# Forgetting attention in a two-layer trunk: page loads spread over two heads' iterations each, and all loads of the loop issued by SyncE

## The chip, the cores and the metric

The kernel runs on one core of a Trainium2 chip. The metric is the device time of one execution in microseconds (us), lower is better. Five engines matter here: TensorE (PE, matmuls and transposes), VectorE (DVE), ScalarE (ACT), GpSimd (POOL) and SyncE (SP, which only issues DMAs here). DMAs can be issued by SP, ACT or POOL; each of these engines works through its own instructions in order, so that an instruction that waits holds up everything behind it on the same engine. The transfers themselves run on 16 DMA engines.

## What is computed

One inference step of a decoder with two layers, for a prompt of 512 tokens and a group of 8 sample sequences with 4 new tokens each. Every layer is a feed-forward block, a mixer and another feed-forward block; the first layer's mixer is gated linear attention, the second's is forgetting attention (FoX) with 16 heads of 64. Only the FoX attention is touched. Its prompt half and its sample half are:

```python
def fox_prompt_attend(q, k, v, logf):          # per block of 128 queries
    s = einsum('bqhd,bkhd->bhqk', qi, k) * HD ** -0.5
    s = s + (Fi[:, :, :, None] - Ft[:, :, None, :])       # F = cumsum(logf)
    s = where(kpos <= qpos, s, -inf)
    return einsum('bhqk,bkhd->bqhd', softmax(s), v)

def fox_paged_attend(q, k_new, v_new, logf_new, cache_k, cache_v, cache_logf, page_table):
    kp = cache_k[page_table]                   # 2 pages of 128 tokens per sequence
    vp = cache_v[page_table]
    ...
    p = softmax(concat([s_past, s_new]))
    return p[..., :P] @ vp + p[..., P:] @ v_new
```

## The kernel before

The kernel is written with a tile framework: the program names tiles, each tile belongs to a tag with a fixed number of buffers, and a planner inserts all waits, hands out the buffers of a tag and sets the order of the instructions on each engine from the program's order and from when it thinks each instruction can start. So the order on an engine is close to the program's, with later work pulled ahead where earlier work can't start yet.

The function `fox` (L1159) first makes queries and gates with matmuls (`fg`, the last of these before the loop), and then runs the attention loop (L1388 to L1413) of 18 iterations `i`. Iteration `i` handles prompt head `i`; `kb = i // 2` is the pair of heads that share a 128-row slice of keys and queries. Four iterations make a sample group `p`, with `q = i % 4` counting within it; group `p` covers the sample sequences `b = 2p` and `2p + 1`.

For the prompt heads:

- `pair_loads(kb)` (L1318) loads, for a pair of heads, the values `vq` (from `vscr`, 256 KB, issued by SP), the keys twice into `kd` (from `khscr`, two DMAs of 256 KB, issued by POOL), the low parts of the keys with the decay rows `kl` (74 partitions, 296 KB, from `klscr`, by POOL) and the query-side decay rows `qe` (10 partitions, 40 KB, from `qxscr`, by POOL; named `qx` in the code). `kd`, `kl` and `qe` are of the type float32r, and the sources are float32. It also splits the queries into high and low parts (ACT, POOL).
- `head_probs(hd)` (L1336) makes the scores in PSUM (matmuls `fs`, L1348 to L1350), the row minimum (DVE, L1351), the exponential (ACT, L1352) and the scaling (DVE, L1357).
- `head_turn` (L1360) transposes the probabilities on PE (`pT`) and copies them out; `head_values(kb)` (L1376) multiplies them with `vq` (`fo`), then DVE, ACT and POOL turn the result into the high and low parts for the output projection (POOL: `ul`, L1385).

For the sample sequences:

- `pair_keys(p, s2)` (L1219) loads the two key pages of one sequence (`kp`, 512 KB each) and its two value pages (`vp`, 512 KB each), both by SP, transposes the key pages on PE (`kpT`), copies the transposes to SBUF (DVE, ACT), and returns a function `scores` that does the score matmuls `sp` (L1262).
- `pair_softmax` (L1266), `pair_probs` (L1281, transposes `spT`), `pair_values` (L1291, matmuls `so` that read `vp`) and `pair_out` (L1309) follow.

The buffers that decide when a load may start: tag `hi` has 6 buffers. One is held through the loop by the sample queries; every `kd` takes one, from its load to the last `fs` of its two heads; every `pair_keys` takes two for the transposed pages `kpT`, until its `scores`. Tag `lo` has 6, four of them held by the gates, so two remain for the `kp` of one sequence. Tag `raw` has 4: the `vp` of one group. `vq`, `kl` and `qe` have two buffers each. All these buffers are given back by PE instructions.

In the loop of the kernel before, a group's `pair_keys` run at `q = 0` and `q = 1`, the scores at `q = 1` and `q = 2`, the softmax at `q = 2`, `pair_probs` at `q = 3` and `pair_values` at the next group's `q = 0`. `pair_loads` for the next pair stands at the start of every even iteration. After the loop comes the output projection `fwo`, whose weights (`rfwo`) take over the `raw` buffers.

Of the kernel before, what the change touches and what calls it, by code (L numbers as in the profile page):

```python
# [9 lines left out]
F32 = mybir.dt.float32  # L10
# [8 lines left out]
P = 128  # L19
D = 1024  # L20
NB = 8
# [29 lines left out]
KX = 74  # L51
# [48 lines left out]
def trunk_kernel(ctx: ExitStack, tc: tile.TileContext, a, out, dbg=None, stop=None):  # L100
    nc = tc.nc
    V, S, G, PE, SP = nc.vector, nc.scalar, nc.gpsimd, nc.tensor, nc.sync
# [17 lines left out]
    def raw_tile(name, dt=F32):  # L120
        return wp.tile([P, 1056], dt, tag="raw", name=name, bufs=4)
# [191 lines left out]
    for k in range(NB):  # L313
        ps = mm_bank(f"xT{k}")
# [6 lines left out]
    ps = mm_bank("xTs")  # L321
# [694 lines left out]
    pages = [SP.value_load(pt[0:1, i:i + 1], min_val=0, max_val=npg - 1) for i in range(16)]  # L1016
# [142 lines left out]
    def fox(after_half):  # L1159
        W = a["fox_w_qg"][0]  # L1160
        with ExitStack() as es:
# [43 lines left out]
            fa = es.enter_context(tc.tile_pool(name="foxa", bufs=1))  # L1205
            xp = es.enter_context(tc.tile_pool(name="foxp", bufs=1, space=bass.MemoryType.PSUM))
            ps = aux_bank("cq")
# [7 lines left out]
            cv = a["cache_v"].rearrange("n t h d -> n t (h d)")  # L1215

            pst = {}

            def pair_keys(p, s2):  # L1219
                if s2 == 0:  # L1220
                    qx = qx2[:, (p % 2) * 512:(p % 2) * 512 + 512]
                    for par in range(2):
                        r = slice(64 * par, 64 * par + 64)
                        for kb in range(2):
                            for i in range(2):
                                o = 16 * kb + 8 * i + 4 * par
                                b = 2 * p + i
                                V.tensor_copy(out=qx[r].rearrange("p (s j k c) -> p s k j c", s=2, j=4, k=2)[:, i, kb, :, o:o + 4],
                                              in_=qTs[r, kb::2, 4 * b:4 * b + 4])
                    ps = xp.tile([P, 512], F32, tag="sp", name=f"sp{p}")  # L1230
                    PE.matmul(ps[:, 0:260], lhsT=cf[:, F_SEL + 128 * p:F_SEL + 128 * p + 128], rhs=nf[:], start=True, stop=False)
                    pst[p] = [qx, ps, []]
                qx, ps, vv = pst[p]
                b = 2 * p + s2
                kr = []
                for g in range(2):
                    t = lo_tile(f"kp{b}_{g}", F32)
                    SP.dma_start(out=t[:, 0:D], in_=ck[bass.ds(pages[2 * b + g], 1)].rearrange("o t d -> t (o d)"))
                    kr.append(t)
                for g in range(2):  # L1240
                    t = raw_tile(f"vp{b}_{g}")
                    SP.dma_start(out=t[:, 0:D], in_=cv[bass.ds(pages[2 * b + g], 1)].rearrange("o t d -> t (o d)"))
                    vv.append(t)
                kt = [hi_tile(f"kpT{b}_{i}", F32)[:, 0:1040].rearrange("p (k c) -> p k c", k=4) for i in range(2)]
                for q in range(4):
                    pk = aux_bank(f"kpT{b}_{q}")
                    for i in range(2):
                        for g in range(2):
                            PE.transpose(pk[:, i * 256 + g * P:i * 256 + (g + 1) * P], kr[g][:, (2 * q + i) * P:(2 * q + i + 1) * P], ident)
                    d = kt[q // 2][:, 2 * (q % 2):2 * (q % 2) + 2, 0:256]  # L1250
                    if q % 2:
                        S.copy(d, pk[:].rearrange("p (k c) -> p k c", k=2))
                    else:
                        V.tensor_copy(out=d, in_=pk[:].rearrange("p (k c) -> p k c", k=2))
                for i in range(2):
                    V.tensor_copy(out=kt[i][:, :, 256:260], in_=kTs[:, 4 * i:4 * i + 4, 4 * b:4 * b + 4])

                def scores():
                    for kb in range(2):
                        for j in range(4):  # L1260
                            c = (s2 * 4 + j) * 2 + kb
                            PE.matmul(ps[32 * j:32 * j + 32, 0:260], lhsT=qx[:, 32 * c:32 * c + 32], rhs=kt[j // 2][:, 2 * (j % 2) + kb],  # L1262
                                      start=False, stop=s2 == 1 and kb == 1)
                return scores

            def pair_softmax(p):  # L1266
                qx, ps, vv = pst[p]
                x = tmp.tile([P, 260], F32, tag="acc", name=f"sx{p}", bufs=2)
                sm = fa.tile([P, 4], F32, tag="sm", name=f"sm{p}", bufs=2)
                V.tensor_tensor_reduce(out=x[:], in0=ps[:, 0:260], in1=cf[:, F_NEWM:F_NEWM + 260], scale=1.0, scalar=-3.0e38, op0=ALU.add, op1=ALU.max, accum_out=sm[:, 0:1])  # L1270
                c = cq[:, p:p + 1]
                V.tensor_tensor(out=sm[:, 1:2], in0=sm[:, 0:1], in1=c, op=ALU.add)
                V.tensor_tensor(out=sm[:, 2:3], in0=c, in1=sm[:, 1:2], op=ALU.subtract)
                S.activation(x[:], x[:], AF.Exp, bias=sm[:, 2:3], accum_out=sm[:, 3:4])
                V.reciprocal(out=sm[:, 0:1], in_=sm[:, 3:4])
                V.tensor_scalar(out=x[:], in0=x[:], scalar1=sm[:, 0:1], scalar2=None, op0=ALU.mult)
                xn = tmp.tile([P, 32, 4], F32, tag="acc", name=f"xn{p}", bufs=2)
                V.tensor_tensor(out=xn[:], in0=x[:, 256:260].unsqueeze(1).to_broadcast([P, 32, 4]), in1=cf[:, F_SEQR + 32 * p:F_SEQR + 32 * p + 32].unsqueeze(2).to_broadcast([P, 32, 4]), op=ALU.mult)
                pst[p] += [x, xn]
# [35 lines left out]

            hst = {}

            def pair_loads(kb):  # L1318
                vq = fa.tile([P, 4, P], F32, tag="vq", name=f"vq{kb}", bufs=2)
                SP.dma_start(out=vq[:], in_=vscr[:].rearrange("(t p) d -> p t d", p=P)[:, :, kb * P:(kb + 1) * P])  # L1320
                kd = hi_tile(f"kd{kb}")[:, 0:1024].rearrange("p (e t) -> p e t", e=2)
                for g in range(2):
                    G.dma_start(out=kd[64 * g:64 * g + 64], in_=khscr[kb * P:(kb + 1) * P].rearrange("(e p) t -> p e t", e=2))
                kl = fa.tile([KX, 2, TP], F32R, tag="kl", name=f"kl{kb}", bufs=2)
                G.dma_start(out=kl[:], in_=klscr[2 * kb:2 * kb + 2].rearrange("e p t -> p e t"))
                qx = fa.tile([KX, 2, TP], F32R, tag="qe", name=f"qe{kb}", bufs=2)
                G.dma_start(out=qx[64:KX], in_=qxscr[2 * kb:2 * kb + 2].rearrange("e p t -> p e t"))
                qs = (uh[:, kb, 0:TP], ul[:, kb, 0:TP])
                for e in range(2):
                    r, x = slice(64 * e, 64 * e + 64), slice(64 - 64 * e, 128 - 64 * e)  # L1330
                    S.copy(qs[e][r], qT[r, kb])
                    (G if kb else V).tensor_tensor(out=qs[e][x], in0=qT[r, kb], in1=qs[e][r].bitcast(F32), op=ALU.subtract)
                    S.copy(qx[0:64, e], qT[r, kb])
                hst["v", kb], hst["k", kb] = vq, (kd, kl, qs, qx)

            def head_probs(hd):  # L1336
                kb, hh = divmod(hd, 2)
# [49 lines left out]
            sc_ = {}  # L1387
            for i in range(18):  # L1388
                p, q = divmod(i, 4)
                if i == 0:  # L1390
                    pair_loads(0)
                if i % 2 == 0 and i < 14:
                    pair_loads(i // 2 + 1)
                if i < 16:
                    head_probs(i)
                if p and q == 0:
                    pair_values(p - 1)
                if p < 4 and q == 0:
                    sc_[0] = pair_keys(p, 0)
                if p < 4 and q == 1:  # L1400
                    sc_[0]()
                    sc_[1] = pair_keys(p, 1)
                if i >= 3 and i % 2:
                    head_values((i - 3) // 2)
                if p < 4 and q == 2:
                    sc_[1]()
                    pair_softmax(p)
                if 1 <= i < 17:
                    head_turn(i - 1)
                if p < 4 and q == 3:  # L1410
                    pair_probs(p)
                if p and q == 1:
                    pair_out(p - 1)  # L1413
# [55 lines left out]
```

## Time and profile before

| | |
|---|---|
| runs shown | 2469.25, 2464.47, 2458.25 us; median 2464.47 |
| the profiled execution | 2457.02 us, its span 2455.2 us (1.8 us lie around it) |
| PE busy in it | 2391.8 us, 97% |
| attention loop in it | from 1841.7 us (first `fs`) to 1988.3 us (first matmul of `fwo`): 146.6 us |
| mean granted TensorE clock | 0.987 |

How to read it: the span runs from the first to the last instruction, and all times of the trace count from its start. The time of an engine is its busy time. PE's matmuls overlap in the pipe, so a PE that shows 98% has no gap, but that does not tell its peak. The clock that the throttle grants TensorE is given as a share of full speed. "Idle before" an instruction is put down to what released it last. A DMA's landing is the time from its issue until its semaphore tells that all of it has arrived.

### The profile page before, as it was taken

The numbers are of one execution on the slowest core, as the hardware profiler recorded it, in microseconds if no ns is written. First come the engines' busy times: TensorE is split into PE (matmuls) and PEld (weight loads), VectorE is DVE, ScalarE is ACT, GpSimd is POOL, SyncE is SP. The second block draws the span as 40 slices with busy tenths as digits, with TensorE's granted clock in tenths as the row PEclk, the third lists the DMA queues.
The fourth block names the chain that finished last, engine by engine and source line by source line (L and its number), as shares of the span: only waits on it lengthen the run. The fifth ranks groups of instructions, "written<-read, shape, count | busy, mean of one in ns | idle before, by whom it ended". The sixth has DMA issues, their size and how long they took to land. (4 is left out here: it accounts for less than half of the span.)

```text
span 2455.2 us, 48218 instructions
## 1 busy us (share of the span) xinstructions
PE 2391.8 (97%) x20204; PEld 2244.9 (91%) x20204; DVE 1237.1 (50%) x2823; ACT 783.2 (32%) x1431; POOL 293.0 (12%) x448
## 2 busy tenths in 40 slices
PE   8999999999899999999999999999998899999999
PEld 6999999988879999999879999999895589999999
DVE  6343334547656354444585444434848556444433
ACT  3212222344534222222335222222347444222221
POOL 0000000104301010000220000001325120000000
PEclk8999999999999999999999999999999899999999
DMA  8636444313172636445257322322148642222221
GB/s 296 214 123 223 162 159 157 97 48 93 38 223 71 226 126 232 157 170 170 106 149 221 104 77 85 104 86 70 53 106 206 168 125 77 87 92 90 72 84 55
DMA packets 325519, 319.38 MB, mean 130 GB/s; under 512 B 24607, under 2 KB 276349, under 8 KB 325254
## 3 DMA queue, kind: packets, MB, share of 16 engines
q1 hardware_dynamic: 297958, 293.81, 37.6%
q0 software_dynamic: 13776, 11.87, 2.3%
q10 hardware_dynamic: 13568, 10.62, 1.4%
q8 instruction: 159, 2.61, 0.4%
q14 instruction: 58, 0.48, 0.1%
HBM read 298.17 MB, written 18.38 MB: 129 GB/s over the span
## 5 line engine op out<-in xcount | busy, mean ns | idle before, releaser
L176 PE MATMUL pa<-uh,hua 128*128 128x272 f32 x1408 | 409.9, 291 | 1.6 <-ACT uh L386 1.5
L177 PE MATMUL pa<-ul,hua 128*128 128x272 f32 x1408 | 408.2, 290 | 0.4 <-DVE ul L387 0.2
L178 PE MATMUL pb<-uh,lub 128*128 128x272 f32 x1408 | 407.6, 289 | 0.0
L178 PE MATMUL pa<-uh,lua 128*128 128x272 f32 x1408 | 406.9, 289 | 0.0
L176 PE MATMUL pd<-gh,hwd 128*128 128x272 f32 x1408 | 406.8, 289 | 0.0
L177 PE MATMUL pb<-ul,hub 128*128 128x272 f32 x1408 | 405.8, 288 | 0.0
L176 PE MATMUL pb<-uh,hub 128*128 128x272 f32 x1408 | 405.7, 288 | 0.0
L178 PE MATMUL pd<-gh,lwd 128*128 128x272 f32 x1408 | 405.4, 288 | 0.0
L177 PE MATMUL pd<-gl,hwd 128*128 128x272 f32 x1408 | 405.2, 288 | 0.0
L393 DVE SCALAR_TENSOR_TENSOR h<-pd,mods,h 128x272 f32<-128x272 f32 (+1 forms) x384 | 185.0, 482 | 251.0 <-PE pd L178 249.9
L176 PEld LDWEIGHTS pa<-uh,hua 128*128 128x128 f32 x1408 | 265.8, 189 | 14.5 <-issue 6.0
L177 PEld LDWEIGHTS pa<-ul,hua 128*128 128x128 f32 x1408 | 266.0, 189 | 1.6 <-DVE ul L387 1.6
L176 PEld LDWEIGHTS pd<-gh,hwd 128*128 128x128 f32 x1408 | 265.2, 188 | 1.7 <-issue 1.6
L177 PEld LDWEIGHTS pb<-ul,hub 128*128 128x128 f32 x1408 | 266.3, 189 | 0.0
L178 PEld LDWEIGHTS pb<-uh,lub 128*128 128x128 f32 x1408 | 266.1, 189 | 0.0
L176 PEld LDWEIGHTS pb<-uh,hub 128*128 128x128 f32 x1408 | 266.0, 189 | 0.0
L178 PEld LDWEIGHTS pa<-uh,lua 128*128 128x128 f32 x1408 | 265.8, 189 | 0.0
L177 PEld LDWEIGHTS pd<-gl,hwd 128*128 128x128 f32 x1408 | 265.5, 189 | 0.0
L178 PEld LDWEIGHTS pd<-gh,lwd 128*128 128x128 f32 x1408 | 265.4, 189 | 0.0
L446 DVE TENSOR_TENSOR g<-g,pb 128x272 f32<-128x272 f32 x176 | 77.0, 437 | 349.1 <-PE pb L178 347.7
L157 ACT CAST hua<-rua 128x1024 fp32r<-128x1024 f32 x88 | 92.2, 1048 | 459.9 <-PE pd L177 349.6
L398 POOL TENSOR_TENSOR h<-h,gs 128x32 f32<-128x32 f32 x192 | 70.7, 368 | 1234.2 <-DVE gs L396 1228.8
(497 smaller groups left out, 4176.3 us busy)
## 6 DMA issues: line engine op xcount, KB each, us to landing
adaw<-in_w_ada_dram SPq DMA_DIRECT2D x128, 512.0 KB, 6.2
rua<-in_w_ffn_up_dram SPq DMA_DIRECT2D x88, 512.0 KB, 3.8
rub<-in_w_ffn_up_dram SPq DMA_DIRECT2D x88, 512.0 KB, 3.9
rwd<-in_w_ffn_down_dram SPq DMA_DIRECT2D x88, 512.0 KB, 4.9
adah<-in_w_ada_dram SPq DMA_DIRECT2D x16, 512.0 KB, 7.7
adaw<-in_w_ada_kv_dram SPq DMA_DIRECT2D x16, 512.0 KB, 7.3
s<-in_state_gla_dram SPq DMA_DIRECT2D x16, 512.0 KB, 4.7
kp<-in_cache_k_dram SPq DMA_DIRECT2D x16, 512.0 KB, 4.7
```

Source lines behind the costliest of these rows:

```text
L157: S.copy(hi, src)
L176: PE.matmul(ps, lhsT=wh, rhs=xh, start=first and i == 0, stop=False)
L177: PE.matmul(ps, lhsT=wh, rhs=xl, start=False, stop=False)
L178: PE.matmul(ps, lhsT=wl, rhs=xh, start=False, stop=last and i == n - 1)
L393: V.scalar_tensor_tensor(out=h[:, m, t0:p1], in0=ps[:, 0:n], scalar=mods[:, gate + m, 0:1], in1=h[:, m, t0:p1], op0=ALU.mult, op1=ALU.add)
L398: G.tensor_tensor(out=h[:, m, TP:T], in0=h[:, m, TP:T], in1=st[:], op=ALU.add)
L446: V.tensor_tensor(out=g[:], in0=g[:], in1=pb[:, 0:HA], op=ALU.mult)
```

## The change

- The loads `kd`, `kl` and `qe` are issued by SP instead of POOL. Their destinations are written as float32 (`bitcast`), so that source and destination have one type.
- `vq` leaves `pair_loads`: it is loaded by `value_load`, for pairs 0 and 1 at the start, and then for the next but one pair right after the `head_values` that gives its buffer back.
- The value pages leave `pair_keys`: `pair_pages(p, s2)` loads them one iteration later, at `q = 1` and `q = 3`.
- The second sequence of a group has its `pair_keys` at `q = 2` instead of `q = 1`. Its scores and the group's softmax move from `q = 2` to the start of `q = 3`, ahead of that iteration's `head_probs`. `pair_probs`, `pair_values` and `pair_out` stay where they were.

```diff
-                qx, ps, vv = pst[p]
+                qx, ps, _ = pst[p]
                 b = 2 * p + s2
                 kr = []
                 for g in range(2):
                     t = lo_tile(f"kp{b}_{g}", F32)
                     SP.dma_start(out=t[:, 0:D], in_=ck[bass.ds(pages[2 * b + g], 1)].rearrange("o t d -> t (o d)"))
                     kr.append(t)
-                for g in range(2):
-                    t = raw_tile(f"vp{b}_{g}")
-                    SP.dma_start(out=t[:, 0:D], in_=cv[bass.ds(pages[2 * b + g], 1)].rearrange("o t d -> t (o d)"))
-                    vv.append(t)
...
+            def pair_pages(p, s2):
+                b = 2 * p + s2
+                for g in range(2):
+                    t = raw_tile(f"vp{b}_{g}")
+                    SP.dma_start(out=t[:, 0:D], in_=cv[bass.ds(pages[2 * b + g], 1)].rearrange("o t d -> t (o d)"))
+                    pst[p][2].append(t)
...
+            def value_load(kb):
+                if kb < NB:
+                    vq = fa.tile([P, 4, P], F32, tag="vq", name=f"vq{kb}", bufs=2)
+                    SP.dma_start(out=vq[:], in_=vscr[:].rearrange("(t p) d -> p t d", p=P)[:, :, kb * P:(kb + 1) * P])
+                    hst["v", kb] = vq
+
             def pair_loads(kb):
-                vq = fa.tile([P, 4, P], F32, tag="vq", name=f"vq{kb}", bufs=2)
-                SP.dma_start(out=vq[:], in_=vscr[:].rearrange("(t p) d -> p t d", p=P)[:, :, kb * P:(kb + 1) * P])
                 kd = hi_tile(f"kd{kb}")[:, 0:1024].rearrange("p (e t) -> p e t", e=2)
                 for g in range(2):
-                    G.dma_start(out=kd[64 * g:64 * g + 64], in_=khscr[kb * P:(kb + 1) * P].rearrange("(e p) t -> p e t", e=2))
+                    SP.dma_start(out=kd[64 * g:64 * g + 64].bitcast(F32), in_=khscr[kb * P:(kb + 1) * P].rearrange("(e p) t -> p e t", e=2))
                 kl = fa.tile([KX, 2, TP], F32R, tag="kl", name=f"kl{kb}", bufs=2)
-                G.dma_start(out=kl[:], in_=klscr[2 * kb:2 * kb + 2].rearrange("e p t -> p e t"))
+                SP.dma_start(out=kl[:].bitcast(F32), in_=klscr[2 * kb:2 * kb + 2].rearrange("e p t -> p e t"))
                 qx = fa.tile([KX, 2, TP], F32R, tag="qe", name=f"qe{kb}", bufs=2)
-                G.dma_start(out=qx[64:KX], in_=qxscr[2 * kb:2 * kb + 2].rearrange("e p t -> p e t"))
+                SP.dma_start(out=qx[64:KX].bitcast(F32), in_=qxscr[2 * kb:2 * kb + 2].rearrange("e p t -> p e t"))
...
                 if i == 0:
                     pair_loads(0)
+                    value_load(0)
+                    value_load(1)
                 if i % 2 == 0 and i < 14:
                     pair_loads(i // 2 + 1)
+                if p < 4 and q == 3:
+                    sc_[0]()
+                    pair_softmax(p)
                 if i < 16:
                     head_probs(i)
                 if p and q == 0:
                     pair_values(p - 1)
-                if p < 4 and q == 0:
-                    sc_[0] = pair_keys(p, 0)
                 if p < 4 and q == 1:
                     sc_[0]()
-                    sc_[1] = pair_keys(p, 1)
+                if p < 4 and q % 2 == 0:
+                    sc_[0] = pair_keys(p, q // 2)
+                if p < 4 and q % 2:
+                    pair_pages(p, q // 2)
                 if i >= 3 and i % 2:
                     head_values((i - 3) // 2)
-                if p < 4 and q == 2:
-                    sc_[1]()
-                    pair_softmax(p)
+                    value_load((i + 1) // 2)
```

More of the change, by code (lines that the diff above doesn't have):

```diff
@@ L1333, in pair_loads @@
                     S.copy(qx[0:64, e], qT[r, kb])
-                hst["v", kb], hst["k", kb] = vq, (kd, kl, qs, qx)
+                hst["k", kb] = (kd, kl, qs, qx)
             def head_probs(hd):
```

## The prediction

> **What bounds the kernel now.** I read the page first, for the engine that fills the span, and then the attention loop alone, by stretches.
>
> ```profile
> span 2455.2 us, 48218 instructions
> PE 2391.8 (97%) x20204; PEld 2244.9 (91%) x20204; DVE 1237.1 (50%) x2823; ACT 783.2 (32%) x1431; POOL 293.0 (12%) x448
> PEclk8999999999999999999999999999999899999999
> ```
>
> PE is the bound of the whole program. A gain can only come from places where PE stands still or runs below full clock. Apart from its start the clock row has one 8, in slice 32 of 40, from 1903 to 1964 us, inside the attention loop. I cut the loop at the first scores matmul of every pair of heads and at the two long gaps, in the view of busy time by stretches:
>
> ```profile
> core 0: us, PE busy (x) PEld busy (x) DVE busy (x) ACT busy (x) POOL busy (x), PEclk, DMA share, GB/s
> 1841.70:1870.70 29.00, 23.88 (x159) 14.24 (x158) 25.00 (x74) 22.66 (x57) 21.23 (x20) 1.00 0.79 211
> 1870.70:1890.10 19.40, 19.09 (x152) 11.04 (x150) 15.14 (x46) 11.41 (x31) 5.84 (x6) 1.00 0.63 197
> 1890.10:1901.30 11.20, 11.15 (x89) 7.91 (x88) 9.37 (x37) 8.09 (x24) 3.29 (x6) 1.00 1.18 216
> 1901.30:1908.00 6.70, 0.06 (x1) 0.00 (x0) 1.14 (x4) 2.56 (x7) 3.25 (x3) 0.72 0.53 106
> 1908.00:1930.50 22.50, 22.21 (x161) 14.01 (x162) 14.58 (x43) 9.47 (x26) 3.24 (x4) 0.86 0.62 191
> 1930.50:1940.00 9.50, 9.49 (x80) 6.49 (x78) 8.46 (x35) 7.49 (x23) 2.47 (x4) 1.00 1.23 168
> 1940.00:1946.00 6.00, 0.00 (x1) 0.03 (x1) 2.83 (x3) 2.50 (x7) 3.28 (x3) 0.65 0.46 104
> 1946.00:1968.80 22.80, 22.78 (x161) 14.04 (x162) 13.63 (x41) 8.24 (x24) 0.00 (x0) 0.87 0.40 148
> 1968.80:1988.30 19.50, 19.21 (x161) 10.77 (x159) 13.55 (x46) 12.25 (x31) 2.56 (x2) 1.00 0.31 91
> ```
>
> Three things stand here. PE is idle for 6.7 and 6.0 us, ahead of heads 8 and 12. The stretch behind each gap ran at a clock of 0.86 and 0.87. In the first stretch PE is idle for 5.1 of 29 us, with DVE busy for 25. Elsewhere PE is full. The waits of PE within the loop name the cause of the gaps:
>
> ```profile
> PE fs L1348 <- DMA kd<-khscr: 12.7, 2, 6.7
> ```
>
> So both gaps are the key tile `kd`. Why it came late stands in POOL's instructions in order of time; these are the loads of pair 4 (heads 8, 9) and pair 6 (heads 12, 13):
>
> ```profile
> 1887.59 1.44 POOL L1325 DMA_DIRECT2D kl<-klscr  x1 [13.44 <-PE fs L1350]
> 1889.04 0.57 POOL L1327 DMA_DIRECT2D qe<-qxscr  x1
> 1889.60 0.60 POOL L1323 DMA_DIRECT2D kd<-khscr  x1
> 1892.96 1.29 POOL L1385 TENSOR_TENSOR ul<-og,uh 128x512 fp32r<-128x512 f32 x1 [2.76 <-ACT uh L1384]
> 1894.19 1.90 POOL L1323 DMA_DIRECT2D kd<-khscr  x3
> 1925.52 1.46 POOL L1325 DMA_DIRECT2D kl<-klscr  x1 [20.92 <-PE kpT L1249]
> 1926.98 0.57 POOL L1327 DMA_DIRECT2D qe<-qxscr  x1
> 1927.55 1.21 POOL L1323 DMA_DIRECT2D kd<-khscr  x2
> ```
>
> POOL works in order. The first `kd` stood behind `kl`, which waited 13.4 us for its buffer, and its second half behind `ul`, which waited for ACT: issued at 1894.19, needed at 1901.3, in use at 1908.0. The other stood behind a `kl` that waited 20.9 us: issued at 1927.55, needed at 1940.0, used at 1946.0. So `kd` had 7.1 and 12.4 us and took 13.8 and 18.5.
>
> **The change part by part.** The loads of the loop, as issued within it, with the queues' totals (q0 is POOL's, q1 holds SP's), and the spread of landings for `kd`, `kl` and `kp` in that order:
>
> ```profile
> q1 hardware_dynamic: 17945, 23.47, 39.8%
> q0 software_dynamic: 12288, 6.98, 23.2%
> kp<-in_cache_k_dram SPq DMA_DIRECT2D x16, 512.0 KB, 4.7
> vp<-in_cache_v_dram SPq DMA_DIRECT2D x16, 512.0 KB, 6.8
> kd<-khscr POOLq DMA_DIRECT2D x16, 256.0 KB, 13.5
> kl<-klscr POOLq DMA_DIRECT2D x8, 296.0 KB, 14.1
> vq<-vscr SPq DMA_DIRECT2D x8, 256.0 KB, 11.5
> qe<-qxscr POOLq DMA_DIRECT2D x8, 40.0 KB, 12.5
> ```
>
> ```profile
> DMA to landing us min/median/max: 4.7/13.5/17.7
> ```
>
> ```profile
> DMA to landing us min/median/max: 10.2/14.1/18.0
> ```
>
> ```profile
> DMA to landing us min/median/max: 3.3/4.7/11.8
> ```
>
> *The lead of `kd`.* Buffers of `hi` seem to be handed out in program order. Before, the six went to the sample queries, `kd0`, `kd1` and the transposed pages of sequences 0 and 1, so `kd2` and all later ones came behind two sequences' pages. With the second `pair_keys` at q = 2 the order is `kd0`, `kd1`, sequence 0, `kd2`, sequence 1, `kd3` and so on: `kd2` finds a free buffer ahead of the loop, and later ones take that of the `kd` three pairs earlier. `kd5` would be issued with `kl4`, about 1887.6, for head 10: a lead of two pairs of heads. A pair takes PE 15.3 us (19.4 + 11.2 over two), so `kd` has some 30 us where its slowest landing was 17.7. Both gaps go: **minus 12.7 us**.
>
> *The clock.* Behind each gap PE ran slow: 22.5 x 0.14 = 3.15 us and 22.8 x 0.13 = 2.96 us. The stretch from 1870.7 with the same place in its group took 19.4 us at 1.00, which fits. Without the gaps: **minus 6.1 us**.
>
> *What is late next: `kl` and `qe`.* Their two buffers are freed by the last `fs` of the pair before, so their lead stays: 13.7 us for `kl4` (1887.59 to 1901.3) and 14.5 for `kl6`. Pages at q = 2 even the iterations out, so I expect leads of about 15. The trace has no `kl` issued by SP. From below its landing is bounded by `kp`'s 3.3 us, from above by its own 18.0. I take its fastest on POOL, 10.2: it leaves a queue that took twice the engine time for a megabyte (23.2% for 6.98 MB against 39.8% for 23.47), and its size stays. Then it costs nothing, and at 18.0 it costs 3 to 4 us in some pairs.
>
> The Trainium skill speaks against a gain from moving loads: by its page DMA: Bandwidth & Descriptors, section Issuing engines are not separate DMA queues, all issuers share the same 16 engines, and another issuer saves only sequencer time. The q0 row, with twice the engine time per megabyte, speaks against it here. By the page alone the landings would stay: 17.7 is still inside `kd`'s 30 us, so the sum would be the same but for `kl`, which at 18.0 is the first rival.
>
> *Issue time.* SP takes over 32 DMAs.
>
> ```profile
> L1238 SPq DMA_DIRECT2D kp<-in_cache_k_dram x16: 332/333/1347, 1835.1 to 1954.4; - x16
> L1323 POOL DMA_DIRECT2D kd<-khscr x16: 586/614/706, 1816.9 to 1933.5; - x16
> ```
>
> At 0.33 us that is 11 us of SP in 146.6, while POOL is rid of more than 16 x 0.61 + 8 x 1.44 = 21 us (the 1.44 from POOL's `kl` above). Neither computes on the path: 0. What counts is order: every load now stands behind the buffer waits of all others on SP. These buffers are all given back by PE, in PE's order, so a queue in the order of freed buffers loses nothing. `vq` and `vp` are only moved to where their buffers come free; their users (`fo`, `so`) come a pair of heads or more later: 0.
>
> *DVE and the softmax.* Without the gaps DVE has less time to catch up: in the second group 14.58 + 8.46 + 2.83 = 25.9 us of work in 22.5 - 3.1 + 9.5 = 28.9, that is 90%. The softmax now starts at q = 3 and its transposes follow in the same iteration. For group 0 the chain of waits has its first and last DVE steps here:
>
> ```profile
> 1861.38 0.43 DVE sx L1270
> 1868.48 0.19 DVE xn L1278
> ```
>
> That is 7.3 us with DVE crowded; between the scores and the transposes PE has one head's work, some 7 us by half a pair. If all hides, 0; if each of four groups and the crowded DVE cost about as much as the first stretch lost, 5.1. The full PE of the later stretches is nearer to 0: I take **plus 2 us**.
>
> *The first stretch.* Sequence 1 leaves iteration 1. What a sequence costs PE stands in the loop's groups of instructions (count, busy us, mean ns):
>
> ```profile
> L1249 PE MATMUL kpT<-cst,kp 128*128 128x128 f32 x128 | 19.6, 284 | 1.2 <-DVE kpT L1254 1.2
> L1262 PE MATMUL sp<-kpT,qx 128*32 128x260 f32 x128 | 12.2, 390 | 0.5 <-DVE kpT L1254 0.5
> ```
>
> At best the 5.1 us of idle PE vanish. At worst the idle stays and one sequence's work, (19.6 + 12.2) / 8 = 4.0 us, moves into a full stretch. DVE was busy for 25 of the 29 us, so the heads behind the idle can use the room that sequence 1 leaves, about as much as is moved: I take 0.
>
> Sum: -12.7 - 6.1 + 2 = **-16.8 us**, with the ends -23.9 (all hidden, first stretch filled) and -9.7 (5.1 and 4.0 lost). The profiled execution took 2457.0 us (span 2455.2 and 1.8 around it), which gives 2440.2. It was quicker than all runs shown; their median is 2464.5, and runs of the changed kernel should lie as these do, so I forecast 2464.5 - 16.8 = **2447.7 us**.
>
> **The rivals.**
>
> *`kl` becomes the wait.* `kl` needs 10.2 us at its fastest for 296 KB, where a `kd` of 256 KB landed in 4.7 and a page of 512 KB in 3.3. It seems to run on few of the engines, whoever issues it; and in SP's queue everything behind it on those engines waits, the next `kl` too. At 18.0 the leads of 13.7 and 14.5 are missed by 4.3 and 3.5 us, 8 us in all, and with the clock dips that gaps of this size brought (6.1) 14. The gain shrinks to 3 to 9 us: about **2459**. For it speaks the 10.2, against it that POOL's transfers crowded it. The Trainium skill (DMA: Bandwidth & Descriptors, section Why a DMA increments its semaphore by 16 and not by 1) has the rule behind this: a DMA uses the largest number of engines, at most 16, that divides the outer dimensions of both its sides, for the 74 rows of `kl` 2. By that rule SP's `kl` is no faster in kind; the trace agrees as far as the 10.2 goes.
>
> *The change doesn't do what it says.* The planner sets SP's order from its own clock. Before, SP already stood for long behind one load:
>
> ```profile
> SPq L1320 <- PE fo L1381: 47.9, 6, 12.0
> ```
>
> If a load that waits 12.0 us stands ahead of a `kp` (4.7 to land, so 16.7 in all) or a `kl`, PE waits as it did for `kd`, and two such places eat the gain: about **2464**.
>
> *Slower: one queue in series.* If the loads of SP follow one another on the slowest engines, a pair of heads needs `kl` 10.2 and four pages at 3.3, 23.4 us. PE now spends 18.3 us on a pair with its gaps (146.6 / 8). Six pairs load within the loop: 6 x 5.1 = 31 us more, about **2495**. It turns to slower from 18.3 us a pair. Against it: the loop's loads have 3.2 MB a pair, and at the 216 GB/s of one stretch these take 15 us, the time PE needs.
>
> **How the numbers follow.** My forecast gets 0.57, the wait for `kl` 0.20, the order that doesn't hold 0.14, the series 0.09. Faster or slower by over 0.5% means below 2452.1 or above 2476.8; that is about what a measurement of this kernel can tell from no change. Faster: nearly all of the forecast's cases and a few of the first rival's, 0.57. Slower: the series, 0.09. Same: 0.34. The range goes from the sum's far end less the spread of runs (2440.6 - 4) to the no-change case with its spread: 2437 to 2467, which leaves out the series and a little at either end.
>
> **What would show it.** In the changed profile PE's waits should have no `kd`; the stretches of heads 8 and 12 should follow at a clock of 1.00; `kd` should be issued about two pairs ahead, by SP; DVE's share should rise to about 90%. Wrong would be: PE waiting for `kl`, `qe` or `kp` by more than 3 us at a time, `spT` waiting for DVE or ACT by over 1 us in every group, or SP waits longer than 12 us with a load behind them that PE lacks.

## The result, and the profile after

The changed kernel takes 2488.64 us, median of 6 runs (2486.98 to 2490.81), against 2462.21 us for the kernel before, median of 6 (2458.25 to 2469.25). The ratio is 1.0117, 95% interval 1.0104 to 1.0130: slower by 1.2%. The prediction was 2447.7 us and its range ended at 2467.

The page of the changed kernel, top and clock row:

```profile
span 2486.1 us, 48224 instructions
PE 2409.9 (97%) x20204; PEld 2251.2 (91%) x20204; DVE 1235.7 (50%) x2823; ACT 782.0 (31%) x1431; POOL 265.9 (11%) x416
PEclk9999999989999999999999999999997999999999
```

PE is 18.1 us longer busy with the same 20204 matmuls, and the clock row has a 7 where the attention loop is. The loop now runs from 1847.4 (first `fs`) to 2020.3 us (first matmul of `fwo`): 172.9 us, where it had 146.6. So the loop lost 26.3 us, as much as the medians differ (26.4). The two profiled executions differ by 30.9 us (2487.9 and 2457.0), because the changed one also came 5.7 us later to its loop, with an 8 early in its clock row. That is taken here as spread between executions: the profiled execution of the kernel before was 5.2 us quicker than its median, and the profiles of the kernels below begin their loops anywhere from 1840.6 to 1855.2.

PE's waits within the loop (total, times, longest):

```profile
PE kpT L1245 <- DMA kp<-in_cache_k_dram: 12.5, 6, 4.4
PE fs L1356 <- DMA qe<-qxscr: 10.1, 2, 5.3
```

The `kd` row is gone, as predicted. In its place PE waits for key pages, and in two places for `qe`, by the profile, which puts a wait down to what came last. These are the two places:

```profile
1871.22 0.77 PE L1356 MATMUL fs<-kl,qe 74*128 74x512 f32 x1 [5.27 <-DMA qe<-qxscr]
1920.56 0.79 PE L1356 MATMUL fs<-kl,qe 74*128 74x512 f32 x1 [4.84 <-DMA qe<-qxscr]
```

Each of these matmuls needs `kl` and `qe`, and by the landings in the trace both were late. PE stood ready at 1865.95 and 1915.72; `kl`, issued at 1858.13 and 1907.99, landed at 1870.75 and 1920.21, and `qe`, the 40 KB issued right behind it, 0.3 us later each time. So `kl` alone would have held PE for 4.8 and 4.5 us of these 5.3 and 4.8. The gaps in the view of busy time by stretches:

```profile
core 0: us, PE busy (x) PEld busy (x) DVE busy (x) ACT busy (x) POOL busy (x), PEclk, DMA share, GB/s
...
1865.90:1871.20 5.30, 0.05 (x1) 0.01 (x1) 1.83 (x4) 1.35 (x3) 5.00 (x5) 0.55 0.94 213
...
1915.20:1920.50 5.30, 0.47 (x1) 0.19 (x1) 0.50 (x2) 0.00 (x0) 0.00 (x0) 0.73 0.99 233
...
1980.20:1984.20 4.00, 0.04 (x1) 0.00 (x0) 0.00 (x0) 0.00 (x0) 0.00 (x0) 0.79 1.02 333
...
sum 172.90, PE 142.33 PEld 82.77 DVE 102.15 ACT 84.41 POOL 25.75; mean PE 11.86 PEld 6.90 DVE 8.51 ACT 7.03 POOL 2.15
```

The sum row splits the loss. PE is idle for 30.6 us (172.9 - 142.3) instead of 18.7 (146.6 - 127.9), 11.9 more; and busy for 142.3 us instead of 127.9, 14.4 more. DVE has the same 102 to 104 us of work. Two different losses, then: waiting for DMAs, and matmuls that take longer.

Why the pages are late begins with SP's instructions in order of time, here around one group of loads:

```profile
1876.93 0.34 SPq L1238 DMA_DIRECT2D kp<-in_cache_k_dram  x1
1882.44 0.39 SPq L1324 DMA_DIRECT2D vq<-vscr  x1
1883.15 0.26 SPq L1332 DMA_DIRECT2D kl<-klscr  x1
1883.46 0.52 SPq L1334 DMA_DIRECT2D qe<-qxscr  x1
1884.16 0.37 SPq L1238 DMA_DIRECT2D kp<-in_cache_k_dram  x1
1888.17 1.81 SPq L1266 DMA_DIRECT2D vp<-in_cache_v_dram  x2
1890.02 1.24 SPq L1330 DMA_DIRECT2D kd<-khscr  x2
```

SP's largest wait in the loop is that of `vq` (total, times, longest):

```profile
SPq L1324 <- PE fo L1388: 47.3, 6, 11.9
```

The two key pages of a sequence are 7.2 us apart. The first is issued at 1876.93; then `vq` waits for `fo` to give up its own, `kl` and `qe` follow, and only then the second page is issued. It comes behind `kl` in the queue, and PE uses it at 1896.10, 11.9 us after its issue, at the end of one of the waits above. What happens to the transfers shows in two stretches after such a group, at their DMA share:

```profile
1896.20:1899.20 3.00, 3.00 (x11) 2.22 (x12) 1.91 (x4) 0.58 (x1) 0.00 (x0) 0.50 0.14 52
1920.50:1925.50 5.00, 4.30 (x16) 3.13 (x16) 2.13 (x4) 0.58 (x1) 0.00 (x0) 0.50 0.14 54
```

For 3 and 5 us the 16 engines are busy to 0.14, that is 2.2 engines' worth, at 52 to 54 GB/s: fourteen engines have finished, and two still work through what the queue has left for them. PE's clock is 0.50 in the same stretches.

The trace also records every update of the semaphore that tells of a landing, 16 of them for a page, and they show the two engines load by load. The `kl` issued at 1883.15 has one update at 1883.57 and two more at its end, 1893.13 and 1893.39. The page issued behind it at 1884.16 has 14 of its 16 updates by 1888.25, before PE stood still at 1891.7; the other two come at 1895.73 and 1896.05, and PE goes on at 1896.10. So the page was issued in time for fourteen engines, and two held it up.

### The profile page after: what moved, and what is told of

It is laid out like the page before. It is cut to its first block, busy times and chain, and to the rows that moved or that the text cites. A ratio compares the mean times of both kernels' runs of the same rounds, so it can differ in the third digit from the quotient of the medians.

```text
span 2486.1 us, 48224 instructions
## 1 busy us (share of the span) xinstructions
PE 2409.9 (97%) x20204; PEld 2251.2 (91%) x20204; DVE 1235.7 (50%) x2823; ACT 782.0 (31%) x1431; POOL 265.9 (11%) x416
```

## The experiments

The kernels in one table. Ratios are to the kernel before, timed beside each. Loop, PE busy, `fo` and scores are of the profiled execution: from the first `fs` to the first `fwo`, and the busy time of PE in it, in all and for these two tiles. The last column is PE's wait for DMAs in the loop. The kernel before had medians from 2458.06 to 2462.21 in the five sessions of these runs, so a difference of a few us between medians of different sessions tells nothing by itself; there the ratios decide.

| kernel | median us | ratio (95%) | loop | PE busy | `fo` | scores | DMA waits |
|---|---|---|---|---|---|---|---|
| before | 2462.21 | 1 | 146.6 | 127.9 | 25.5 | 14.8 | 12.7 |
| changed | 2488.64 | 1.0117 (1.0104-1.0130) | 172.9 | 142.3 | 29.5 | 20.5 | 22.6 |
| changed, `kl` cut at 64 | 2459.50 | 1.0003 (0.9992-1.0013) | 144.4 | 132.7 | 27.7 | 19.0 | 0 |
| changed, `kl` cut at 62 | 2484.79 | 1.0101 (1.0080-1.0121) | 172.4 | 142.7 | 27.7 | 19.9 | 20.6 |
| changed, key pages ahead | 2451.50 | 0.9968 (0.9957-0.9979) | 135.1 | 129.1 | 27.2 | 19.1 | 1.6 |
| before, cut at 64 | 2440.29 | 0.9920 (0.9899-0.9940) | 127.2 | 122.0 | 25.1 | 14.8 | 0 |
| changed, `kl` on GpSimd | 2483.67 | 1.0094 (1.0075-1.0114) | 166.1 | 135.6 | 26.6 | 19.1 | 24.4 |
| loads on SP only | 2469.12 | 1.0045 (1.0032-1.0059) | 156.6 | 138.9 | 28.5 | 19.8 | 12.4 |
| schedule only | 2457.88 | 0.9994 (0.9978-1.0009) | 139.8 | 129.9 | 27.8 | 19.8 | 5.0 |
| loads only, cut | 2451.73 | 0.9966 (0.9950-0.9981) | 135.9 | 129.3 | 28.5 | 18.5 | 0 |
| schedule only, cut | 2447.74 | 0.9953 (0.9936-0.9969) | 134.1 | 128.2 | 26.2 | 19.7 | 0 |
| changed, pages ahead, cut | 2459.63 | 0.9993 (0.9980-1.0006) | 142.2 | 133.7 | 28.4 | 19.8 | 0 |
| changed, cut, turned | 2451.61 | 0.9969 (0.9951-0.9988) | 133.3 | 120.8 | 20.8 | 12.4 | 2.6 |
| before, cut, turned | 2438.51 | 0.9906 (0.9887-0.9924) | 125.5 | 118.7 | 21.0 | 13.5 | 0 |
| loads only, cut, turned | 2444.92 | 0.9949 (0.9933-0.9965) | 133.2 | 121.0 | 21.0 | 15.5 | 0 |
| schedule only, cut, turned | 2437.81 | 0.9923 (0.9904-0.9943) | 125.4 | 115.8 | 20.9 | 13.0 | 0 |
| changed, pages ahead, cut, turned | 2446.34 | 0.9952 (0.9935-0.9969) | 130.7 | 118.9 | 21.0 | 13.1 | 0 |

### `kl` in two loads, cut at 64 partitions, and the control at 62

```diff
-                SP.dma_start(out=kl[:].bitcast(F32), in_=klscr[2 * kb:2 * kb + 2].rearrange("e p t -> p e t"))
+                for r in (slice(0, 64), slice(64, KX)):
+                    SP.dma_start(out=kl[r].bitcast(F32), in_=klscr[2 * kb:2 * kb + 2, r].rearrange("e p t -> p e t"))
```

The control has 62 in place of 64: as many loads, the same bytes, but 62 partitions, whose largest divisor up to 16 is 2.

> The changed kernel, with each kl load cut into one of 64 and one of 10 partitions. Theory 'few engines' (a load of 74 rows runs on two of the 16 DMA engines, takes about 10 us there, and every page, vq and kd issued behind it on SP is complete only when those two engines get to it): kl then lands in under 6 us, the 27 us of PE waits for kp and qe fall under 5 us, no clock dips, time 20 to 35 us below the changed kernel, 2450 to 2465. Rival 'order' (SP issues the second page of each key pair only behind a vq load that waits for fo): kl lands sooner, but kp is issued as late as now, PE still waits some 10 us or more for kp, time within 12 us of the changed kernel's 2489.

> Control: the same cut at row 62, into 62 and 12 partitions; as many loads and bytes as with 64 and 10. Theory 'few engines': 62 has with 16 engines no larger common divisor than 2, so 62 rows stay on two engines: kl still lands in 9 us or more, the waits for kp and qe stay at 15 us or more, time 2478 to 2492. If instead a smaller load or the new order on SP is what helps, it comes out with the cut at 64, within 6 us of it.

The cut at 64 takes 29.1 us off the changed kernel; the cut at 62 takes 3.9, which is no more than the 4.2 us by which the kernel before differs between the two sessions, and the intervals of the two ratios overlap. With the cut at 62 the waits are still there, and SP's own wait for a `kl` to land shows (second fence, from SP's waits):

```profile
PE fs L1357 <- DMA qe<-qxscr: 12.1, 3, 5.8
PE kpT L1245 <- DMA kp<-in_cache_k_dram: 8.5, 5, 3.9
```

```profile
SPq L1330 <- DMA kl<-klscr: 20.4, 3, 8.6
```

With the cut at 64, PE waits for no DMA in the loop. The 64 rows of its first `kl` in the loop, issued at 1856.99, landed at 1860.57: 3.6 us, where the whole one took 12.6. In the quiet stretches behind its groups of loads the two busy engines are gone too, which had stood at 0.14 for as long:

```profile
1908.00:1913.00 5.00, 5.00 (x39) 3.15 (x35) 3.43 (x17) 3.29 (x11) 0.00 (x0) 1.00 0.06 15
1892.00:1896.00 4.00, 4.00 (x32) 2.60 (x32) 2.66 (x11) 2.02 (x7) 0.00 (x0) 1.00 0.04 14
```

So the number of partitions in a load, not the number of loads or bytes, made the waits. The Trainium skill (DMA: Bandwidth & Descriptors, section Why a DMA increments its semaphore by 16 and not by 1) gives 2 engines for 74 and for 62 rows and 16 for 64. The traces agree: a share of 0.14 of 16 for the 74 rows, two late updates for a part of 62 rows (issued at 1883.64, updates at 1892.82 and 1894.15), and all 16 updates of a part of 64 rows within 0.8 us (1859.80 to 1860.57).

But the loop still had 144.4 us, and PE was busy for 132.7 of them: the second loss stays.

### The key pages ahead of `vq`, `kl` and `qe`

`key_loads` holds the two page loads that stood at the top of `pair_keys`, and is called one sequence ahead.

```diff
                 if p < 4 and q % 2 == 0:
                     sc_[0] = pair_keys(p, q // 2)
+                    key_loads(i // 2 + 1)
```

> The changed kernel, with the two key pages of the next sequence loaded right behind the transposes that free their buffers, ahead of vq, kl and qe in the program. Theory 'order': both pages are issued together and in time, the 12.5 us of PE waits for kp go, and with them three of the clock dips, time 15 to 20 us below the changed kernel, about 2470. Theory 'few engines': the kp waits shrink too, as the pages now stand ahead of kl, but kl and qe come behind them and PE waits for qe or kl as now (10 us) or longer; time 2475 to 2490.

It gave more than either theory expected: 37.1 us off. `kl` is whole here and is still issued by SP, and the two engines still run on alone behind it:

```profile
1887.00:1892.00 5.00, 5.00 (x52) 3.39 (x49) 4.52 (x14) 1.84 (x6) 0.00 (x0) 1.00 0.15 51
```

PE is busy through all of it. The loads that follow `kl` in the queue are now those that nobody needs soon. `kl` itself is no faster, 11.9 to 17.1 us from issue to landing in the loop, but the planner's new order on PE also uses it later: 13.2 to 18.9 us after its issue, where in the changed kernel PE stood ready for it after 7.8 and 7.7 us in two pairs. So it takes both: a load on two engines, and a user that comes soon, its own or that of a load behind it. How much of the 37.1 us comes from the pages and how much from the later use of `kl` this run doesn't separate.

### The same cut in the kernel before

```diff
-                G.dma_start(out=kl[:], in_=klscr[2 * kb:2 * kb + 2].rearrange("e p t -> p e t"))
+                for r in (slice(0, 64), slice(64, KX)):
+                    G.dma_start(out=kl[r], in_=klscr[2 * kb:2 * kb + 2, r].rearrange("e p t -> p e t"))
```

> The kernel before, with each kl load, still issued by POOL, cut into 64 and 10 partitions. Theory 'few engines': kl on POOL is slow for the same reason (10.2 us at its fastest) and kd stands behind it on the same two engines; cut, kl lands in under 7 us, kd in under 9, and the 12.7 us of PE waits for kd fall under 4; time 10 to 18 us below the kernel before. Rival 'order' (kd came late because POOL issued it late): kd for heads 8 and 12 still arrives late by 4 us or more each, time within 8 us of the kernel before.

2440.29 us, against 2458.06 for the kernel before in the same session: this edit of two lines brings 17.8 us, a little more than the whole change was forecast to. Landings of the kernel before with the cut, from the view of DMA issues:

```profile
kd<-khscr POOLq DMA_DIRECT2D x16, 256.0 KB, 5.0
vq<-vscr SPq DMA_DIRECT2D x8, 256.0 KB, 3.1
kl<-klscr POOLq DMA_DIRECT2D x8, 256.0 KB, 4.3
kl<-klscr POOLq DMA_DIRECT2D x8, 40.0 KB, 4.1
qe<-qxscr POOLq DMA_DIRECT2D x8, 40.0 KB, 4.3
```

They were 13.5 (`kd`), 11.5 (`vq`), 14.1 (`kl`) and 12.5 (`qe`). `vq` came from SP's queue and gained as much as the loads of GpSimd's: the two engines are shared by both queues. And the loop's 12.7 us of waits for `kd` go although in GpSimd's queue a `kd` still stands behind a `kl` that waits for its buffer:

```profile
1920.20 1.16 POOL L1326 DMA_DIRECT2D kl<-klscr  x2 [10.89 <-PE kpT L1249]
1921.36 1.20 POOL L1323 DMA_DIRECT2D kd<-khscr  x2
```

The two engines had left their mark in the kernel before as well. Of the second half of the `kd` for head 8, issued at 1894.19, 14 updates had come by 1901.1, and PE became ready for it at 1901.3; the last two came at 1907.12 and 1907.93, and PE went on at 1908.0. The stretch behind the second gap has them too:

```profile
1946.00:1951.00 5.00, 5.00 (x18) 3.85 (x19) 2.40 (x7) 1.00 (x2) 0.00 (x0) 0.50 0.15 41
```

### `kl` alone back on GpSimd's queue, uncut

```diff
-                SP.dma_start(out=kl[:].bitcast(F32), in_=klscr[2 * kb:2 * kb + 2].rearrange("e p t -> p e t"))
+                G.dma_start(out=kl[:], in_=klscr[2 * kb:2 * kb + 2].rearrange("e p t -> p e t"))
```

> The changed kernel with the kl load alone back on GpSimd's queue, uncut. If kl harms the pages and qe because it stands in the same queue ahead of them, the waits for kp and qe mostly go: 2456 to 2466, like the kernel with the cut. If it harms them because it fills engines that they need too, whichever queue it comes from, they stay: 2478 to 2490.

The time is that of the second case, but the wait is neither's: PE now waits for `kl` itself, and not for pages.

```profile
PE fs L1356 <- DMA kl<-klscr: 24.4, 3, 9.4
```

```profile
kp<-in_cache_k_dram SPq DMA_DIRECT2D x16, 512.0 KB, 10.1
kl<-klscr POOLq DMA_DIRECT2D x8, 296.0 KB, 15.5
```

`kp` lands in 10.1 us, twice its 4.7 before, though no `kl` stands in its queue, and `kl` takes 15.5. So the harm doesn't come from the queue's order alone: loads of both queues slow each other on the engines that they share, and here another queue for `kl` only changed which load was late.

### Each half of the change alone, without and with the cut

"Loads only" is the kernel before with `kd`, `kl` and `qe` on SP; "schedule only" is the changed kernel with these three on GpSimd.

> The kernel before, with kd, kl and qe issued by SP and nothing else of the change. Theory 'few engines': kl and the pages now share SP's queue, pages wait behind kl on its two engines as in the changed kernel, PE waits 15 to 30 us for kp, qe or kl, time 2470 to 2490. Rival 'schedule' (the new places of pages, values and the second sequence are what costs): no new waits, kd issued without POOL's detours, time 2440 to 2458.

> The changed kernel, with kd, kl and qe issued by POOL as before; the new places of vq, vp, the second sequence and the softmax stay. Theory 'few engines': the pages are free of kl's queue, so PE's waits for kp go, and kd is issued a pair earlier, so its waits go too; what is left is the third theory, 'torn pairs': in the new order PE's fo matmuls run as 2 + 14 and sp as 2 + 8 + 6 instead of 16 in a row, so that matmuls on different columns of the array no longer run side by side, some 1.0 us per fo and 0.7 us per sp group, 10 to 13 us over the loop. Time 2450 to 2465. Rival 'schedule': as slow as the changed kernel, 2480 or more.

> The kernel before with kd, kl and qe on SP and each kl cut into 64 and 10 partitions. 'Few engines': no DMA waits of PE over 1 us, the old PE order with fo and sp mostly in one row, time as with the cut on POOL, 2436 to 2446. If SP's single queue itself costs something, it lies 5 us or more above that.

> The new schedule with kd, kl and qe on POOL and kl cut into 64 and 10. No DMA waits. Against the kernel before with the same cut (2440) this shows the schedule alone: 'torn pairs' expects 8 to 15 us more, 2448 to 2455, with PE's busy time in the loop some 10 us above that kernel's 122. If the order on PE doesn't matter, 2440 give or take 4.

Uncut, the loads alone cost 0.45%, with 12.4 us of waits where 15 to 30 were expected, and the schedule alone changes nothing that can be told; together they cost 1.17%, more than the sum. The schedule brings the `kd` lead that was predicted (no wait for `kd`), and SP's queue puts `kl` ahead of the pages of this schedule. With the cut neither half waits for a DMA, and yet both stay behind the kernel before with the same cut: 11.4 and 7.5 us. What they share is PE's busy time, 129.3 and 128.2 us against 122.0. The new order on PE is thus not the schedule's alone: the loads on SP bring it too.

### The torn groups, and turning them round

PE's timeline of the changed kernel with the cut at 64 shows what the extra busy time is. Columns: start, duration, instruction, count; each matmul is two instructions here.

```profile
1900.17 1.07 PE L1389 MATMUL fo<-pt,vq 128*64 128x512 f32 x2
...
1906.09 0.62 PE L1258 MATMUL sp<-kpT,qx 128*32 128x260 f32 x2
...
1907.56 0.65 PE L1258 MATMUL sp<-kpT,qx 128*32 128x260 f32 x8
...
1908.67 0.64 PE L1258 MATMUL sp<-kpT,qx 128*32 128x260 f32 x6
1909.24 2.37 PE L1389 MATMUL fo<-pt,vq 128*64 128x512 f32 x14
```

The program writes 16 instructions in a row for each. `fo` uses half of the array's columns per matmul and the scores a quarter, and neighbours on different columns run side by side: 8 of the scores take 0.65 us, 2 take 0.62. The planner pulled the first ones ahead, as soon as the operand of the first head or of the first page was ready, so that one half or one quarter of the array works alone. The Trainium skill (TensorEngine Tiling (Array Packing), section Tiling Modes) says that different tiles can run in parallel; the trace agrees for the 8 in 0.65 us, and adds that a tile with no such neighbour in PE's order takes nearly as long as four together.

The turn lets each group begin with the operand that is ready last:

```diff
-                        for j in range(4):
+                        for j in (3, 2, 1, 0):
...
-                    for hh in range(2):
+                    for hh in (1, 0):
```

> The changed kernel with the cut at 64, and with the order inside two groups of matmuls turned round, so that the operand that is ready last comes first: the two halves of fo (hh 1, then 0) and the four tiles of the scores (j 3 to 0). Without a DMA wait that kernel was still 17 us over the kernel before with the same cut (loop 144.3 against 127.2; TensorE busy 132.6 against 122.0, of it fo 27.7 against 25.2 and the scores 19.0 against 14.8). The theory of torn groups expects fo at 25 to 26 and the scores at 15 to 16.5 us in the loop, and 2447 to 2454 in all. The rival, that the torn groups only fill time in which TensorE would have waited for VectorE, expects the busy time to fall and the idle time to rise by as much: 2457 to 2462.

> The kernel before with the cut at 64, and with the same turn inside fo and the scores. There the groups were whole already in the loop (fo 25.2, scores 14.8), so the theory of torn groups expects almost nothing: 2436 to 2443. The rival, that the turned order costs or gains something by itself, by starting each group later, expects 3 us or more to either side of 2440.3.

> The changed kernel with both cures at once: the two key pages of the next pair loaded right behind each other, and the kl load cut at 64 partitions. Either cure alone already left almost no DMA wait in the loop (2459.5 with the cut, 2451.5 with the key pages ahead). The theory that both cure the same wait expects that they do not add up: 2446 to 2453, with no DMA wait of TensorE in the loop and TensorE's busy time in the loop still 128 to 133 us. The rival, that each takes away a cost of its own (27 and 37 us), expects below 2440.

PE's timeline of the changed kernel with cut and turn:

```profile
1920.25 1.08 PE L1258 MATMUL sp<-kpT,qx 128*32 128x260 f32 x16
1921.26 1.08 PE L1389 MATMUL fo<-pt,vq 128*64 128x512 f32 x4
...
1922.78 1.51 PE L1389 MATMUL fo<-pt,vq 128*64 128x384 f32 x12
```

Now 4 of `fo` take 1.08 us, where 2 alone took 1.07. PE's busy time in the loop fell by 11.9 us (132.7 to 120.8), its idle time rose by only 0.8 (11.7 to 12.5), and the median fell by 7.9: the theory of torn groups holds against its rival. `fo` and the scores fell further than expected, to 20.8 and 12.4 us: the theory had taken the kernel before as whole. In the kernel before the expectation was wrong in one point: its groups were partly torn too (`fo` 25.1 to 21.0). But there the time moved by 1.8 us, within the intervals (0.9899 to 0.9940 and 0.9887 to 0.9924): 3.3 us of busy time went, and half of it came back as idle time.

The key pages ahead together with the cut missed its expectation: at 2459.63 it is no better than the cut alone and 8.1 worse than the key pages alone, without any DMA wait. Its PE was busy for 133.7 us, 4.6 more than with the key pages alone. Since the program's text differs only in the cut, the planner's order is the suspect, and the next runs test it.

### Each half, and all of it, with the groups turned round

> The kernel before with only the three loads on SP, with the kl cut at 64, and with fo and the scores turned round. Without the turn it stood at 2451.7, that is 11.4 above the kernel before with the same cut on GpSimd's queue (2440.3). If what is left is torn groups alone, it comes to 2437 to 2444. If SP's queue itself costs something, it stays 6 us or more above 2440.

> The changed kernel with its three loads back on GpSimd, the kl cut at 64, and the turn. Without the turn it stood at 2447.7. If the two heads' iterations cost only by tearing groups, 2437 to 2443, the same as the kernel before with both cures (2438.5). If the later place of the softmax and of the second sequence costs idle time of its own, as the 12.5 us of idle TensorE in the changed kernel with cut and turn suggest, 2444 to 2450.

> The changed kernel with all three cures: cut at 64, key pages of a sequence behind each other, and the turn. With the first two it stood at 2459.6, no better than with the cut alone, and with TensorE busy for 133.7 us in the loop. If that is torn groups again, busy falls to 119 to 123 us and the time to 2440 to 2450, below the 2451.6 of cut and turn alone, in which key pages still cost 2.6 us of waits. If the key pages ahead cost something else when the cut is there, it stays above 2453.

The loop of the three, in this order, each from its own profile:

```profile
1841.70:1974.87 133.17, 121.01 (x955) 72.72 (x954) 100.03 (x323) 83.89 (x223) 25.74 (x20) 0.99 0.60 185
```

```profile
1840.56:1965.95 125.39, 115.79 (x954) 71.48 (x954) 102.07 (x323) 84.16 (x223) 43.02 (x50) 1.00 0.69 196
```

```profile
1844.88:1975.56 130.68, 118.92 (x955) 70.53 (x954) 101.64 (x323) 84.22 (x222) 26.04 (x20) 1.00 0.60 188
```

The schedule alone comes to 2437.81 us, the same as the kernel before with both cures (2438.51; intervals 0.9904 to 0.9943 and 0.9887 to 0.9924). So in sum the two heads' iterations are worth nothing and cost nothing that can be told: PE is 2.9 us less busy (115.8 against 118.7) and 2.8 us longer idle (9.6 against 6.8). The third kernel confirms the suspicion on the missed one: busy time 133.7 to 118.9, median 13.3 us lower.

SP's queue is another matter. The loads alone stay 6.4 us above the kernel before with both cures (the ratios, 0.9949 and 0.9906, are further apart), which lies between the two expectations, and the changed kernel with all three cures 8.5 us above the schedule alone. No DMA is waited for there; most of it is idle time of PE, 12.2 us against 6.8 (133.2 - 121.0, 125.5 - 118.7). PE's largest waits in the loop of the loads alone:

```profile
PE kpT L1249 <- DVE kpT L1254: 3.6, 4, 1.4
PE pT L1367 <- DVE kpT L1254: 2.6, 4, 1.5
```

PE waits for DVE's copies, where the kernel before with both cures has 0.5 and 1.3 us of these waits, while DVE has the same work (100.0 us against 99.5). Why these copies come later when SP issues the loads was not tried; the order on PE and DVE differs between the two kernels, so the planner is the likely place, but that is argued, not shown. The best three kernels of this study, all with `kl` on GpSimd and cut at 64 (the kernel before with the cut, with cut and turn, and the schedule alone with both), beat the kernel before by 0.8 to 0.9%.

## Why the prediction was wrong

- **`kd`'s lead, minus 12.7**: right. SP issues the `kd` of pair 5 at 1911.06, right behind the `kl` of pair 4, and PE's waits have no `kd` row. The cause that stood behind it was only half right, though: the prediction put the lateness down to GpSimd's order, and the cut in the kernel before removes the same wait while `kd` still stands behind a waiting `kl` there. What made a `kd` take 13.8 and 18.5 us was the `kl` beside it, on two engines.
- **The clock, minus 6.1**: the size was right. The kernel before with the cut does the same work in 122.0 us of busy PE at clock 1.00, instead of 127.9 at 0.93: 5.9 us. But new gaps brought new dips. The changed kernel has about 9.6 us of them (142.3 against 132.7 with the cut, without the gaps), at a mean clock of 0.89 in the loop.
- **"Then it costs nothing", for `kl` at 10.2 us**: this step failed, twice over. First, `kl` itself came late. The prediction expected leads of about 15 us in every pair; they were uneven, 7.8 and 7.7 us in pairs 2 and 4, where PE's order has the first matmul of the new pair early, and 14 to 25 in the others. And SP's `kl` landed in 10.0 to 13.6 us, not in 10.2. In pairs 2 and 4 it missed PE by 4.8 and 4.5 us; these are 9.3 of the 10.1 us that the profile puts down to `qe`. Second, what `kl` costs the loads behind it on its two engines was left out: the waits for `kp`, 12.5 us.
- **"A queue in the order of freed buffers loses nothing"**: this step failed too. The order in which buffers come free is not the order in which the loads are needed: `vq`, whose wait for `fo` is up to 11.9 us, is needed a pair of heads later, and the second key page behind it at once. It cost so much only together with `kl`: with the cut at 64 the order of the loads in the program is the same, and PE waits for none of them. With `kl` whole, moving the key pages ahead is worth 37.1 us, though the later use of `kl` on PE has a share in it that isn't measured.
- **DVE and the softmax, plus 2; the first stretch, 0**: with the groups turned round the schedule alone has the loop of the kernel before with the same cures (125.4 and 125.5 us): 0 together, of 2.8 us more idle and 2.9 us less busy PE.
- **PE's busy time**: a step that the prediction didn't have. It took the work of PE as given; the planner's new order made it about 10.7 us longer (132.7 against 122.0, both near full clock and without DMA waits). `fo` and the scores alone have 6.8 of that (2.6 and 4.2), and with the groups turned round 2.1 are left (120.8 against 118.7), so torn groups are most of it, 7 to 9 us.
- **The rivals**: the rival on `kl` (2459) had the cause, few engines and everything behind it waiting. Its 8 us of waits for `kl` are near the 9.3 us that `kl` was late, but they came from short leads and not from a landing of 18.0 us, and it gave the loads behind `kl` no price. The prediction's own sign of being wrong, waits for `kl`, `qe` or `kp` of more than 3 us, came four times (5.3, 4.8, 4.4 and 4.0). The time came nearest to that of one queue in series (2495), and the loop did rise to 21.6 us a pair of heads (172.9 / 8). The mechanism of the series, the sum of `kl` and four pages, is not what happened: with the key pages ahead every one of these loads is still in one queue, and the loop takes 135.1 us.

The sum as it came: 11.9 us more idle PE, of it 9.9 for DMAs (22.6 against 12.7); 14.4 us more busy PE, of it about 10.7 the new order on PE, torn groups for the most part, and the other 3.7 the deeper clock dips. Together 26.3. The split of the busy time is an estimate: it takes the order on PE to be the same with and without the cut.

## What to carry to other kernels

Look at the partition count of every load before its bytes: here one load of 74 rows held up all others on its engines, and cutting it at 64 brought more than a new schedule. In a queue, order loads by when they are needed, not by when their buffers come free, and ask of a slow load who stands behind it, not only whether it is in time itself. When an edit changes a planner's order, compare PE's busy time for the same instructions: if it moves, see whether matmuls that share the array still stand together.

## What the runs showed of the hardware that was not expected

- A load of 74 partitions on SP's queue left work on two of the 16 DMA engines when the others had finished (share 0.14, 52 to 54 GB/s; 14 of the 16 updates of a page behind it 4.1 us after its issue, the last 11.9); on GpSimd's it landed in 14.1 us and its 64-row part in 4.3. It slows loads of the other queue as well: `vq` on SP's queue landed in 11.5 us with it and 3.1 without.
- A matmul on a quarter of the array's columns takes nearly as long alone (2 instructions, 0.62 us) as four of them side by side (8 instructions, 0.65 us); one on half the columns takes 1.07 us alone and two take 1.08.
